# Head transposes six pieces behind their block, and the second attention's multiplication four steps behind its scores

## The chip, the cores and the metric

The kernel runs on one core of a Trainium2 chip. The metric is the device time of one execution in microseconds, given as the median of several runs. In the profile PE is TensorE's matmuls, PEld its weight loads, DVE is VectorE, ACT is ScalarE, POOL is GpSimd, and SP is SyncE, whose queue issues nearly all DMAs.

## What is computed

One encoder block over 256 tokens of width 1024, in float32. The reference, cut to what matters:

```python
h = rmsnorm(x, norm_mix_g)
qkv_a, q_b, k_b, v_b, gate_logits = split(h @ w_in)             # 7424 columns
for gi, (window, dil) in enumerate(((128, 1), (512, 4), (2048, 16))):   # mixer A, 8 heads of 64 each
    qg = partial_rope(rmsnorm(q[gi], qn_a[gi]), pos)
    kg = partial_rope(rmsnorm(k[gi], kn_a[gi]), pos)
    og, lg = dilated_window_attention(qg, kg, v[gi], window, dil)
o_a = sum over groups, weighted by softmax of the denominators
o_b = gqa_blocked_attention(axial_rope(rmsnorm(q_b)), axial_rope(rmsnorm(k_b)), v_b)   # mixer B, 8 on 2 heads
merged = sigmoid(g_a) * (o_a @ w_proj_a) + sigmoid(g_b) * (o_b @ w_proj_b)
x = x + merged @ w_out
x = x + moe_ffn(rmsnorm(x, norm_ffn_g), ...)     # top 4 of 32 experts: 1024 -> 2 x 1024 -> 1024, clamped SwiGLU
```

The experts' weights are 32 x (1024 x 2048 + 1024 x 1024) floats, 402.7 MB; the other matrices are some 42 MB. Each weight is read once.

## The kernel before

**Two parts.** A front part normalises, projects, runs both attentions, merges and routes. Then a loop over 32 experts (line 1266) multiplies the gathered tokens of each expert with its weights as they arrive.

**Steps.** All matmuls with weights in the front part are cut into 76 pieces (lines 840 to 845), one a step. `prep` (line 464) splits a piece's weights into a high and a low part, one ScalarE copy and one VectorE subtraction (`split`, line 375, lines 376 and 377), two steps ahead of use; `run_piece` (line 860) multiplies. The blocks of w_in come in the order v0 kvb k0 q0 k1 q1 k2 q2 v2 v1 qb, four pieces of two 128-rows each (steps 0 to 43; lines 501, 502 and 504 are the matmuls), then 16 gate pieces (44 to 59), 8 projection pieces (60 to 67, lines 489, 490 and 492) and 8 of w_out (68 to 75).

**Tasks.** Everything else is a task with a due step. `later(d, fn)` (line 449) sets one d steps ahead; `run_tasks` (line 453), called ahead of each piece (lines 943 to 956), runs those that are due, in the order of due step and number. So an engine's order is the program's order, written out by steps.

**Key and query heads.** When a key or query block of mixer A is through, `headnorm` (line 511) evicts its two token halves on ScalarE (lines 520 and 521), sums squares on VectorE (522), takes the root on GpSimd (525) and applies the rotary tables there (530 to 535). LAT - 1 steps later VectorE scales each half (line 549), and LAT steps later `qk_epilogue` (line 558) has `transpose_heads` (551) run four 128x128 transposes for each half on TensorE (554) with one ScalarE eviction (555). After the second half the work tile `hn` is dropped (line 568). LAT is 5 (line 509). The heads of mixer B have counts of their own, LATQ and LATK.

**Attentions.** `unit_a` and `unit_b` (lines 657 and 720) each return three tasks: scores with their softmax, transposes of the probabilities (line 640, evicted at 641), and the multiplication with v (`pv`). `schedule_units` (line 769) sets them LAG = (0, 2, 3) steps behind the unit's start. Mixer B's eight units start at steps 53 to 60; its `pv` acts for every second unit, at steps 57, 59, 61 and 63 (line 758). After the fourth and the eighth unit `finish_o` (line 649) evicts the result as a high part on ScalarE (654) and a low part on VectorE (655); the projection of mixer B (pieces 64 to 67) reads it. From step 59 on ScalarE also runs two sigmoids a step for the gates (line 787), and switches its function table between them and the exponentials (line 741).

**Buffers and weights.** Large tiles come from 9 pairs of 1 MB halves (`bigt`, line 135, takes the half that has been free longest; `drop`, line 151, gives back). `pump` (line 299) issues weight loads on SP's queue in order whenever a half is free, at most three chunks ahead until the first attention is done and without a limit after that; a load waits in that queue until the last user of its half is through. The first 20 chunks of the experts are 1 MB each and are fetched in the order FETCH (line 28); they are consumed in the order 0, 1, 2, ... where two neighbours that share a pair give it back together. A later chunk needs a whole pair.

Of the kernel before, what the change touches and what calls it, by code (L numbers as in the profile page):

```python
# [24 lines left out]
N_PAIR, N_ONE = 9, 6  # L25
HALVED, LENT = 2, (1, 2)
BD = 8
FETCH = (1, 12, 4, 16, 6, 5, 2, 3, 10, 7, 11, 13, 0, 14, 15, 8, 17, 9, 18, 19)
RA, RB = 0.7, 1
WU = (6, 10, 2, 0, 0)  # L30
CAP2 = 3
LAG = (0, 2, 3)
W = (2, 1, 2, 4)
SENT = -3.0e38
MARK = 3.0e38
# [44 lines left out]
def hybrid_moe_block(ctx: ExitStack, tc: tile.TileContext, x, norm_mix_g, w_in, b_gate, qn_a, kn_a, qn_b, kn_b,  # L80
# [54 lines left out]
    def bigt(shape, dt=F32, name="b"):  # L135
        n = -(-math.prod(shape[1:]) // SLOT)
        part = [(a, p) for p in halves if p[2] == dt for a, v in zip(p[3], p[1]) if v is None]
        stamp[0] += 1
        age, p = min(part, key=lambda t: t[0], default=(0, None))
        if n == 2 or not part:  # L140
            assert n_pairs[0] < N_PAIR, (name, step, nxt, use, reserve)
            n_pairs[0] += 1
            age, p = 0, [big.tile([128, 2 * SLOT], dt, name=nm(name), tag="big"), [None, None], dt, [0, 0]]
            halves.append(p)
        h = next(i for i in range(2) if p[1][i] is None and p[3][i] == age)
        p[1][h:h + n] = [True] * n
        t = view(p[0][:, h * SLOT:(h + n) * SLOT], shape)
        where[id(t)] = (t, p, h, n)
        return t

    def drop(*tiles):
        for t in tiles:
            _, p, h, n = where.pop(id(t))
            if p is None:
                n_ones[0] -= 1
                continue
            p[1][h:h + n] = [None] * n
            p[3][h:h + n] = [stamp[0]] * n
            if p[1] == [None, None]:
                halves[:] = [q for q in halves if q is not p]  # L160
                n_pairs[0] -= 1
# [10 lines left out]
    def ps(tag, shape=(128, 512), name=None):  # L172
        bufs = {"g": 3, "s": 2, "t": 2, "o": 1}[tag]
        return psum.tile(list(shape), F32, name=nm(tag), tag=tag, bufs=bufs)
# [116 lines left out]
    fetch = list(range(len(chunks)))  # L291
    fetch[n_dense:n_dense + len(FETCH)] = [n_dense + i for i in FETCH]
    nxt = [0]
# [152 lines left out]
    tasks = []  # L446
    step = [0]

    def later(d, fn):
        uid[0] += 1  # L450
        tasks.append((step[0] + d, 10 + uid[0], fn))
# [54 lines left out]

    kqT = {}
    vt = {}
    LAT, LATQ, LATK = 5, 9, 8

    def headnorm(pss, nh, t1_, t2_, rot, dst, post, lat=LAT):

# [35 lines left out]
    def scaled(c, y, r, nh):  # L548
        V.tensor_mul(y, y, r[:, :, None].to_broadcast([128, nh, HD]))

    def transpose_heads(src, dst, nblk):
        pt = ps("t")
        for j in range(nblk):
            PE.transpose(pt[:, j * 128:(j + 1) * 128], src[:, j * 128:(j + 1) * 128], ident)
        S.activation(dst, pt[:, :nblk * 128].rearrange("p (j t) -> p j t", j=nblk), AF.Copy)


    def qk_epilogue(which, g):
        def ep(pss):
            if g not in kqT:  # L560
                kqT[g] = bigt([128, 2, 4, T], name="kqT")
            w = 0 if which == "q" else 1

            def post(c, y, hn):
                later(LAT, lambda: transpose_heads(y.rearrange("p h d -> p (h d)"),
                                                   kqT[g][:, w, :, c * 128:(c + 1) * 128], 4))
                if c == 1:
                    later(LAT, lambda: drop(hn))
            headnorm(pss, 8, lambda c: tabA1[:, w, g, c, :], lambda c: tabA2[:, w, g, c, :], 8,
                     lambda c, y, r: scaled(c, y, r, 8), post)  # L570
        return ep
# [194 lines left out]
                    reserve[0] -= 2  # L766
        return scores, lambda: softmax_t(st), pv

    def schedule_units(units, first, every):
        for n, u in enumerate(units):  # L770
            for j in (0, 2, 1):
                tasks.append((step[0] + first + int(n * every) + LAG[j], (2, 0, 1)[j] + 1000000, u[j]))


    gates = {}
# [107 lines left out]
    units_b = [unit_b(i, c) for c in range(2) for i in range(4)]  # L883
    units_a = [unit_a(hp, c, u) for c in range(2) for hp in range(4) for u in range(2)]
    A0, B0 = max(at["v", 1], at["v", 2]) + 2, at["gate", 0] + 9
# [5 lines left out]
    later(14, rstd_row)  # L891
    later(22, fold_router)
    later(18, expert_bias)
    schedule_units(units_a, A0, RA)
    schedule_units(units_b, B0, RB)
    later(at["proj", 0, 0], hT_done)
    for j in range(8):
        later(at["proj", 0, 0] + j - 1, lambda j=j: gate_sigmoid(j))
# [44 lines left out]
    for i in range(NP + AHEAD - 2):  # L943
# [10 lines left out]
        j = step[0] = i - AHEAD  # L954
# [45 lines left out]
    first = Pair()  # L1000
# [265 lines left out]
    for e in range(n_exp):  # L1266
        p = e // 2
# [34 lines left out]
    with tc.If(most > CAP):  # L1302
        with tc.For_i(0, E, 1) as e:
# [11 lines left out]
            for blk in range(1, T // CAP):  # L1315
# [8 lines left out]
                xT, y = fxy[:, 0, :512].rearrange("p (k s) -> p k s", k=8), fxy[:CAP, 1]  # L1324
# [66 lines left out]
```

## Time and profile before

| | us |
|---|---|
| three runs | 1206.65, 1202.38, 1204.87 |
| median | 1204.87 |
| the profiled execution, its own time | 1208.11 |
| its span | 1206.3 |
| TensorE matmul busy | 1131.8 (94%) |
| VectorE busy | 394.7 (33%) |
| ScalarE busy | 270.6 (22%) |
| GpSimd busy | 104.4 (9%) |
| HBM read 444.01 MB | 369 GB/s over the span |

The span is what the profile covers; the time of the execution is 1.8 us longer. Matmuls overlap, so a busy TensorE is not one at its peak. A row of the timeline gives the start and the length of a group of instructions, its engine and line, the tiles written and read, the shape and count, and in brackets how long the engine stood before it and for what. The clock is the share of TensorE's full speed that was granted.

### The profile page before, as it was taken

The page shows a single profiled execution, that of the slowest core. Times are in us where ns is not written, and L with a number is a line of the kernel's source. Part 1 is how long each engine was busy: PE and PEld are TensorE (multiplying, and loading weights), DVE is VectorE, ACT ScalarE, POOL GpSimd, SP SyncE. Part 2 cuts the span into 40 slices and gives each one's busy share as a digit, 9 for nine tenths or more (in the row PEclk, how much of TensorE's full clock was granted, in tenths as well). Part 3 has the DMA queues.
Part 4 walks back from the last instruction along what each step waited for, and adds up shares of the span by engine and source line. Part 5 has one row for each costly group of instructions (what it writes and reads, how often), then busy time and mean ns, then how long its engine had stood idle before and what let it go on. Part 6 is the DMA issues. An engine that isn't in the chain of part 4 may idle for free.

```text
span 1206.3 us, 14307 instructions
## 1 busy us (share of the span) xinstructions
PE 1131.8 (94%) x5956; PEld 573.5 (48%) x5956; DVE 394.7 (33%) x845; ACT 270.6 (22%) x473; POOL 104.4 (9%) x119
## 2 busy tenths in 40 slices
PE   8999999999999999999989898989898989899996
PEld 6777789897434344343434242324243423233333
DVE  4766576564223222232222131212222222222122
ACT  5644555763111101111011101010101010101011
POOL 4767140010000000000000000000000000000000
PEclk9999999999999999999999999999999999999999
DMA  8724417389999999999999999999999999999995
GB/s 302 267 105 154 160 37 277 143 318 373 399 430 430 430 430 432 429 431 432 430 431 430 431 430 430 431 432 429 431 429 432 431 430 431 430 431 431 430 429 205
DMA packets 59628, 446.03 MB, mean 370 GB/s; under 512 B 5356, under 2 KB 17928, under 8 KB 33928
## 3 DMA queue, kind: packets, MB, share of 16 engines
q1 hardware_dynamic: 59224, 444.41, 88.8%
q8 instruction: 49, 0.80, 0.2%
q10 hardware_dynamic: 336, 0.66, 0.2%
q14 instruction: 19, 0.16, 0.0%
HBM read 444.01 MB, written 1.05 MB: 369 GB/s over the span
## 4 chain that ended last, share of the span: by engine, by line
DMA 49%; PE 38%; POOL 6%; issue 3%; ACT 3%; DVE 2%; ACTq 0%; POOLq 0%; SPq 0%; DVEq 0%
DMA w<-in_w_down_dram 26%; DMA w<-in_w_gate_up_dram 23%; PE g L1137 14%; PE o L1177 6%; PE s L1195 2%; PE g L489 2%; PE g L490 2%; PE g L492 2%; POOL hrs L525 1%; PE s L1110 1%; PE t L1157 1%; POOL w L530 1%; PE g L502 1%; PE g L501 1%; POOL hz L533 1%
## 5 line engine op out<-in xcount | busy, mean ns | idle before, releaser
L1137 PE MATMUL g<-w,pair 128*64 128x512 f32 x2008 | 450.5, 596 | 26.9 <-DMA w<-in_w_gate_up_dram 26.0
L1137 PEld LDWEIGHTS g<-w,pair 128*64 128x64 f32 x2008 | 137.9, 137 | 310.6 <-issue 264.9
L1177 PE MATMUL o<-w,act 128*64 128x512 f32 x992 | 222.1, 596 | 27.7 <-DMA w<-in_w_down_dram 27.6
L1160 DVE TENSOR_TENSOR gu<-t,biasT 128x256 f32<-128x256 f32 x128 | 45.4, 417 | 428.1 <-PE t L1157 428.1
L1177 PEld LDWEIGHTS o<-w,act 128*64 128x64 f32 x992 | 70.0, 137 | 167.0 <-issue 117.4
L1147 ACT ACTIVATE gu<-g 128x512 f32<-128x512 f32 x64 | 38.2, 597 | 408.9 <-PE g L1137 399.7
L1185 ACT ACTIVATE pair<-o 64x512 f32<-64x512 f32 x62 | 36.6, 591 | 283.3 <-PE o L1177 282.8
L1112 DVE TENSOR_TENSOR pair<-s,gT 128x512 f32<-128x512 f32 x30 | 20.8, 692 | 184.8 <-PE s L1110 184.8
L377 DVE TENSOR_TENSOR whl<-w,whl 128x1024 fp32r<-128x1024 f32 (+1 forms) x60 | 73.7, 1254 | 18.3 <-ACT whl L376 17.9
L501 PE MATMUL g<-whl,hTh 128*128 128x512 f32 (+1 forms) x176 | 70.0, 400 | 0.7 <-ACT whl L376 0.5
L502 PE MATMUL g<-whl,hTh 128*128 128x512 f32 (+1 forms) x176 | 68.4, 391 | 0.0
L1110 PEld LDWEIGHTS s<-selr,xa 128*128 128x128 f32 x480 | 57.7, 196 | 12.2 <-issue 12.2
L1110 PE MATMUL s<-selr,xa 128*128 128x128 f32 x480 | 60.5, 285 | 0.0
L376 ACT ACTIVATE whl<-w 128x1024 fp32r<-128x1024 f32 (+1 forms) x60 | 59.7, 1039 | 2.6 <-PE g L504 1.7
L1195 PE MATMUL s<-pair,gT 128*128 128x512 f32 x120 | 56.9, 606 | 0.0
L1196 DVE TENSOR_TENSOR acc<-s,acc 128x512 f32<-128x512 f32 x56 | 38.7, 692 | 29.9 <-PE s L1195 29.9
L504 PE MATMUL g<-whl,hTh 128*128 128x512 f32 (+1 forms) x176 | 45.9, 383 | 0.0
L1157 PEld LDWEIGHTS t<-cf,gu 128*128 128x128 f32 x256 | 33.3, 210 | 26.0 <-issue 26.0
L1157 PE MATMUL t<-cf,gu 128*128 128x128 f32 x256 | 39.4, 297 | 0.0
L501 PEld LDWEIGHTS g<-whl,hTh 128*128 128x128 f32 x176 | 33.9, 193 | 8.7 <-ACT whl L376 1.3
L502 PEld LDWEIGHTS g<-whl,hTh 128*128 128x128 f32 x176 | 34.0, 193 | 6.1
L504 PEld LDWEIGHTS g<-whl,hTh 128*128 128x128 f32 x176 | 32.9, 192 | 6.7
(280 smaller groups left out, 981.6 us busy)
## 6 DMA issues: line engine op xcount, KB each, us to landing
w<-in_w_gate_up_dram SPq DMA_DIRECT2D x120, 2048.0 KB, 38.8
w<-in_w_down_dram SPq DMA_DIRECT2D x60, 2048.0 KB, 38.7
w<-in_w_in_dram SPq DMA_DIRECT2D x22, 1024.0 KB, 8.3
w<-in_w_gate_up_dram SPq DMA_DIRECT2D x11, 1024.0 KB, 9.4
w<-in_w_down_dram SPq DMA_DIRECT2D x6, 1024.0 KB, 9.6
w<-in_w_in_dram SPq DMA_DIRECT2D x6, 512.0 KB, 8.3
P<-in_w_in_dram SPq DMA_DIRECT2D x3, 1024.0 KB, 6.3
P<-in_w_gate_up_dram SPq DMA_DIRECT2D x3, 1024.0 KB, 7.7
```

The source lines that it names most:

```text
L376: S.activation(dst_h, src, AF.Copy)
L377: V.tensor_sub(dst_l, src, f(dst_h))
L501: PE.matmul(pss[c][:, :n], lh[:, k, cols], h[:, q, :], start=(k == 0), stop=False)
L502: PE.matmul(pss[c][:, :n], ll[:, k, cols], h[:, q, :], start=False, stop=False)
L504: PE.matmul(pss[c][:, :n], lh[:, k, cols], l[:, q, :], start=False, stop=(k == nk - 1))
L1110: PE.matmul(pg[:, j * 128:(j + 1) * 128], xa[:, c, run_cols(k, GU)], q.selr[:, c].rearrange("p a s -> p (a s)"), start=(c == 0), stop=(c = ...
L1137: PE.matmul(g1[j][u * 64:(u + 1) * 64, :], a, w[:, k - k0, u * FF + j * 512:u * FF + (j + 1) * 512], start=(k == 0), stop=(k == 7))
L1157: PE.transpose(pt[:, j * 128:(j + 1) * 128], gu[:, run_cols(k, DN)], ident)
L1160: V.tensor_add(t[:, 4 * b:4 * b + 4, :], p4[:, :, u, :], bias[:, u * 8 + 4 * b:u * 8 + 4 * b + 4, :].to_broadcast([128, 4, CAP]))
L1177: PE.matmul(po[u * 64:(u + 1) * 64, :], act[:, k, :], w[:, k - k2, u * 512:(u + 1) * 512], start=(k == 0), stop=(k == 7))
L1195: PE.matmul(pc, q.gT[:, c * 128:(c + 1) * 128], q.ysb[:, sl], start=True, stop=True)
L1196: V.tensor_add(acc[0][:, c, sl], pc, base[:, c, sl])
```

## The change

The transposes of mixer A's key and query heads, their evictions and the freeing of `hn` come six steps behind the block (a new constant LATT); the scaling in front of them keeps its step. The multiplications of mixer B come four steps behind the unit's start (58, 60, 62 and 64); mixer A's stay at three. Eight of the 20 entries of FETCH stand in another order.

```diff
-FETCH = (1, 12, 4, 16, 6, 5, 2, 3, 10, 7, 11, 13, 0, 14, 15, 8, 17, 9, 18, 19)
+FETCH = (1, 2, 4, 16, 6, 3, 5, 12, 10, 7, 11, 13, 0, 14, 15, 8, 17, 9, 18, 19)
-LAG = (0, 2, 3)
+LAG = ((0, 2, 3), (0, 2, 4))
...
-    LAT, LATQ, LATK = 5, 9, 8
+    LAT, LATT, LATQ, LATK = 5, 6, 9, 8
...
             def post(c, y, hn):
-                later(LAT, lambda: transpose_heads(y.rearrange("p h d -> p (h d)"),
+                later(LATT, lambda: transpose_heads(y.rearrange("p h d -> p (h d)"),
                                                    kqT[g][:, w, :, c * 128:(c + 1) * 128], 4))
                 if c == 1:
-                    later(LAT, lambda: drop(hn))
+                    later(LATT, lambda: drop(hn))
...
-    def schedule_units(units, first, every):
+    def schedule_units(units, first, every, lag):
         for n, u in enumerate(units):
             for j in (0, 2, 1):
-                tasks.append((step[0] + first + int(n * every) + LAG[j], (2, 0, 1)[j] + 1000000, u[j]))
+                tasks.append((step[0] + first + int(n * every) + lag[j], (2, 0, 1)[j] + 1000000, u[j]))
...
-    schedule_units(units_a, A0, RA)
-    schedule_units(units_b, B0, RB)
+    schedule_units(units_a, A0, RA, LAG[0])
+    schedule_units(units_b, B0, RB, LAG[1])
```

## Rows read from the trace of the kernel before

**Rows 1.** Busy us by engine in two stretches, granted clock, DMA share, GB/s.

```profile
295.00:300.00 5.00, 5.00 (x26) 1.72 (x24) 0.00 (x0) 0.00 (x0) 0.00 (x0) 1.00 0.66 213
540.00:1190.00 650.00, 595.46 (x2796) 230.06 (x2794) 144.07 (x331) 72.16 (x124) 0.00 (x0) 1.00 1.01 429
```

**Rows 2.** SP queue's own waits, 0 to 330 us: sum, times, longest.

```profile
SPq L314 <- PE g L1137: 24.1, 6, 7.8
```

**Rows 3.** Timeline of TensorE, head transposes (L554) and ends of weight pieces (L504).

```profile
54.69 0.63 PE L554 MATMUL t<-cf,w 128*128 128x128 f32 x4 [1.14 <-DVE w L549]
...
82.72 0.63 PE L554 MATMUL t<-cf,tabs 128*128 128x128 f32 x4 [0.85 <-DVE tabs L549]
84.43 0.63 PE L554 MATMUL t<-cf,tabs 128*128 128x128 f32 x4 [1.08 <-DVE tabs L549]
...
95.80 1.03 PE L554 MATMUL t<-cf,w 128*128 128x128 f32 x8
...
101.22 1.07 PE L504 MATMUL g<-whl,hTh 128*128 128x512 f32 x4
103.94 1.07 PE L504 MATMUL g<-whl,hTh 128*128 128x512 f32 x4
...
108.35 0.63 PE L554 MATMUL t<-cf,w 128*128 128x128 f32 x4 [0.63 <-PE g L504]
110.12 0.63 PE L554 MATMUL t<-cf,w 128*128 128x128 f32 x4 [1.14 <-DVE w L549]
```

**Rows 4.** Busy us by engine around three waits; the third number from the end is the clock.

```profile
52.00:55.00 3.00, 1.86 (x12) 1.29 (x11) 1.98 (x3) 2.38 (x5) 1.74 (x4) 1.00 0.00 1
107.00:115.00 8.00, 6.24 (x25) 4.67 (x24) 6.77 (x8) 6.23 (x9) 5.72 (x5) 0.79 0.74 249
234.00:242.00 8.00, 6.20 (x44) 5.46 (x43) 4.76 (x9) 7.91 (x14) 0.00 (x0) 0.79 0.00 0
```

**Rows 5.** Timeline of GpSimd, head normalisation of blocks k0, k2 and q2.

```profile
47.42 1.29 POOL L530 TENSOR_TENSOR w<-w,tabs 128x512 f32<-128x512 f32 x1
...
50.00 2.28 POOL L530 TENSOR_TENSOR w<-w,tabs 128x512 f32<-128x512 f32 x1
...
98.97 3.97 POOL L525 TENSOR_TENSOR hrs<-hss,mhalf 128x16 f32<-128x16 f32 x1 [3.65 <-DVE hss L524]
...
111.45 3.85 POOL L525 TENSOR_TENSOR hrs<-hss,mhalf 128x16 f32<-128x16 f32 x1 [2.20 <-DVE hss L524]
```

**Rows 6.** Timeline of VectorE, the two scalings of block k2.

```profile
106.49 1.76 DVE L549 TENSOR_TENSOR w<-w,hrs 128x512 f32<-128x512 f32 x1 [1.04 <-POOL w L535]
109.28 0.69 DVE L549 TENSOR_TENSOR w<-w,hrs 128x512 f32<-128x512 f32 x1 [1.03 <-POOL w L535]
```

**Rows 7.** Timeline of TensorE, multiplication of units 4 and 5 (L758), projection halves (L492).

```profile
234.80 0.43 PE L758 MATMUL o<-P,vb 128*64 128x128 f32 x2
237.03 1.88 PE L758 MATMUL o<-P,vb 128*64 128x128 f32 x14 [1.80 <-ACT P L641]
...
248.06 0.64 PE L492 MATMUL g<-oT,whl 128*128 128x256 f32 x4
249.50 0.64 PE L492 MATMUL g<-oT,whl 128*128 128x256 f32 x4
```

**Rows 8.** DMA issues by tile: count, KB each, median us to landing.

```profile
w<-in_w_in_dram SPq DMA_DIRECT2D x22, 1024.0 KB, 8.3
```

**Rows 9.** Timeline of VectorE: low part of the first result, last unit's scaling.

```profile
229.65 0.69 DVE L655 TENSOR_TENSOR oT<-o,oT 128x512 fp32r<-128x512 f32 x1 [1.85 <-ACT oT L654]
...
239.54 0.62 DVE L745 TENSOR_SCALAR tabs<-tabs,mzb 128x256 f32<-128x256 f32 x2
```

**Rows 10.** Timeline of ScalarE: first result's eviction, table loads for units 6 and 7.

```profile
229.03 0.59 ACT L654 ACTIVATE oT<-o 128x512 fp32r<-128x512 f32 x1
231.02 1.28 ACT L741 ACT_TABLE_LOAD   x1 [1.40 <-DVE mzb L739]
...
237.00 1.28 ACT L741 ACT_TABLE_LOAD   x1
```

## The prediction, on record before the result

> **What bounds the kernel now.** I read the stretches first. From 540 to 1190 us the DMA engines are full (share 1.01, 429 GB/s) while TensorE stands 54 of 650 us [rows 1]: the experts' 402.7 MB set that part, and a change in front of it pays only if it brings forward the moment from which the weights run without a break. That moment hangs on TensorE: the last break is at 295 to 300 us (213 GB/s, so 2.5 us of weights lost) [rows 1], and the DMA queue's own waits show why: it stood six times, 24.1 us in all, until the first experts' matmuls gave buffers back [rows 2]. So the front part, up to the first expert matmul, counts nearly one to one as long as TensorE paces it. There I read TensorE's timeline for what it stands for, and find two places that the diff touches.
>
> The first is the query/key heads. A weight piece of 512 columns takes 2.72 us (101.22 to 103.94) [rows 3]. The head transposes of the three key blocks wait for VectorE's scaling: 1.14 us at 54.69, 0.85 and 1.08 at 82.72 and 84.43, 0.63 and 1.14 at 108.35 and 110.12 [rows 3]; the eight at 95.80, of a query block, ran in one go behind key block k2's last matmul. After the third wait the clock fell: 0.79 over 107 to 115, a loss of (1 - 0.79) x 8 = 1.68 us, from the 2.4 to the 1.2 GHz level and back; after the first it did not (1.00 over 52 to 55) [rows 4]. What they wait for is GpSimd: block k2 starts there at 98.97 and ends when VectorE's last scaling can start, at 109.28 [rows 5, 6].
>
> The second is the second attention. Its third probability multiplication starts at 234.80, stands 1.80 us for ScalarE's eviction of transposed probabilities, and goes on at 237.03 [rows 7]; over 234 to 242 the clock is 0.79, again 1.68 us [rows 4].
>
> **Part 1, LATT 5 to 6.** Twelve groups of transposes (two token halves of six blocks), their ScalarE evictions and the freeing of hn move one piece later; their count does not change. The scaling stays where it is (lat is unchanged), so VectorE's and GpSimd's order stays. Removed: the waits, 1.14 + 0.85 + 1.08 + 0.63 + 1.14 = 4.84 us; per key block another 0.23 because two groups of four (0.63 each) become one of eight (1.03), so 0.69; and the clock's 1.68. That is 7.2 us.
>
> What is late next: k2's heads are ready some 14.2 us after its block's last matmul: 3.2 from 95.80 until GpSimd starts at 98.97, 10.3 on GpSimd until 109.28, 0.69 of scaling [rows 3, 5, 6]. Five pieces and one block's transposes give 5 x 2.72 + 0.8 = 14.4: covered, by 0.2. A query block's reductions stand behind the key block's last scaling in VectorE's order, so its GpSimd work starts 2.2 us after the key block's (the wait at 111.45) [rows 5]: ready 14.2 + 2.2 + 10.3 = 26.7 after the key block's end, against nine pieces and two blocks' transposes, 26.1. I leave 0.6 us of waiting in sum. Bounds: nothing left (-7.2), or only the one piece won (-2.7, a rival below). Taken: **-6.6 us**, since GpSimd's dates come forward with the matmuls that feed it.
>
> ScalarE: the evictions now stand one weight split later; nobody waits on them but the scores of step 38, a whole piece (2.72) after q2's transposes. SP: hn's slot comes free one piece later, and two w_in chunks are loaded into such slots (those for steps 30 and 42); they land 8.3 us after issue [rows 8], and six or more steps (over 16 us) lie between. Following bigt, drop and pump by hand, every w_in chunk gets the slot that it had. Cost: nothing; if that cover were gone, up to one piece.
>
> **Part 2, LAG of the second attention 3 to 4.** The four multiplications move from steps 57, 59, 61, 63 to 58, 60, 62, 64. Removed: the wait of 1.80 and the clock's 1.68 at step 61, 3.48 us. Step 61 goes straight from 234.8 into its piece, two halves of 1.44 (248.06 to 249.50) [rows 7], and is through at 237.7.
>
> Added, first: step 62 opens with the transposes of the last unit's probabilities, and these are scaled only at 239.54 + 0.62 = 240.16 [rows 9]. Does this date come forward? ScalarE is the pace there: one round from one exponential's table load to the next takes 237.00 - 231.02 = 5.98 us [rows 10]. The move takes the eviction of 0.59 at 229.03 and the 1.40 that the exponentials stood (they waited for a reduction queued on VectorE behind L655) out of step 59 [rows 9, 10], and puts both into step 60, in front of the last unit's exponentials: unit 6 gets 2 us earlier, unit 7 stays. So TensorE, which came to these transposes behind that date before, now stands **2.5 us** (237.7 to 240.16), with the third multiplication and the piece of step 62 queued behind. Bounds 0.5 (both ScalarE savings reach unit 7) to 2.7.
>
> Second: the last multiplication stands at step 64, right in front of the first projection that reads its result. From the eviction's start to the end of the low part on VectorE is 229.03 to 229.65 + 0.69, 1.31 us [rows 9, 10], with the hand-overs **1.4 us**, which before lay beside step 63's piece. Bounds 1.3 to 2.5 (a weight split of one us ahead on ScalarE).
>
> The clock: two waits. The only long ones of the trace, 1.77 in two parts and 1.80, cost 1.68; those of 1.14 and of 0.85 with 1.08 cost nothing [rows 3, 4]. I let it fall after the 2.5 (1.68) and not after the 1.4. Bounds 0 and 3.36. Part 2: 2.5 + 1.4 + 1.68 - 3.48 = **+2.1 us**.
>
> **Part 3, FETCH and the slots.** P slots come free one step later, so the prefetched expert chunks choose other slots. By hand: chunk 1 as before; chunk 2 takes the slot of the first projection chunk, 4 and 16 the slots that they had, then 6, 3, 5, 12, 10, and the pairs end as (2,3), (4,5), (6,7), (10,11), (12,13), each with both halves consumed together. Before step 64 is over, eight one-MB chunks are issued either way; the last four depend on step 64's multiplication instead of 63's and come within some 0.5 us of their old place, with over 10 us of transfers queued in front of them. Zero; if the cover fails, 1 MB at 429 GB/s, 2.4 us, which the break at 295 us could hold [rows 1].
>
> **Sum.** -6.6 + 2.1 = -4.5 us in the profiled execution (span 1206.3, own time 1208.11: 1203.6). The median of the runs, 1204.87, is 3.2 below that execution; I put the same sum on it: **1200.4**.
>
> **Rivals.** (a) *GpSimd keeps the pace*: only latency is bought, its blocks keep their dates, and by step 38 TensorE is ahead by the one piece put before the last transposes: -2.7 + 2.1, 1204.3. For it: GpSimd works 2 x 10.3 us in a pair of blocks, and waits of 2.2 and 3.65 us are its only gaps [rows 5]. Against: the 3.65 is a wait for the matmuls. (b) *The second attention costs nothing*: no clock fall, 2.5 + 1.4 - 3.48 = +0.4, so -6.2, 1198.7. For: waits of 1.14 left the clock alone. Against: 2.5 is the longest of all. (c) *The gain stops at the weights*: if the chunks' dates do not follow, only the 2.5 us break closes: 1202.4. Against: the queue's waits are for matmuls [rows 2]. (d) *Slower: GpSimd stretches*. Its 512-wide multiply took 1.29 at 47.42 and 2.28 at 50.00 [rows 5], and VectorE's scaling 1.76 at 106.49 beside a busy GpSimd, 0.69 at 109.28 beside an idle one [rows 6]: they hinder each other. If splits now fall beside both multiplies of a block, that is 2.0 us a block, 8.0 over k1, q1, k2, q2, all of it waited for: -6.6 + 8.0 + 2.1 = +3.5, 1208.4. It decides from 1.1 us a block (4.5 / 4). Against: VectorE's order is unchanged, and k2 took its 10.3 us with splits beside it. The Trainium skill, GPSIMD Engine Reference, section 1 (Specifications), speaks for (d): GpSimd's SBUF interfaces are shared with VectorE and contend with VectorE instructions that have two SBUF inputs; by that rule, these rows agree.
>
> **Numbers.** Forecast 0.47 (1198.9 to 1202.0), (b) 0.20, (a) 0.17, (c) 0.08, (d) 0.08. Range 1197.4 to 1204.4: it leaves out (d), a part of (a), and the far side of (b). About 0.3%, 3.6 us, is what a measurement of this kernel tells from no change, so 1201.25 is the line: of the forecast 0.7 lies beyond it, of (b) nearly all, of (a) and (c) little: faster 0.54; slower 0.08 from (d); same 0.38.
>
> **What would show it.** Right: no VectorE waits over 0.5 us at L554, granted clock 1.00 through 107 to 115, the scores of step 38 some 6 to 7 us earlier; a wait of about 2.5 us at the last unit's transposes instead of 1.8 at a multiplication, 1.4 us at step 64, the first expert matmul some 4.5 us earlier. Wrong: GpSimd's blocks at their old dates (a), clock 1.00 past step 62 (b), a longer break of the DMA around 295 (c), GpSimd blocks over 11.4 us (d).

## The result and the profile after

| | median | runs | ratio to before, 95% |
|---|---|---|---|
| before | 1204.72 us (1202.38 to 1206.65) | 6 | |
| after | 1196.32 us (1195.35 to 1199.64) | 6 | 0.9934 [0.9923, 0.9946] |
| before, later | 1202.22 us (1201.39 to 1205.66) | 11 | |
| after, later | 1196.44 us (1196.18 to 1198.26) | 6 | 0.9946 [0.9932, 0.9960] |

The change is worth 8.0 us (1 - 0.9934 of 1204.7), with 6.5 to 9.3 in the interval, and 6.5 us in the later comparison, with 4.8 to 8.2 in the interval; the two medians of after agree within 0.2 us, so what differs is before's. The forecast was 4.5 us. The median lies 1.1 us under the low end of the range; the sign was right.

The two first profiles may not be subtracted. Their spans differ by 12.0 us (1206.3 and 1194.3), of which 3.5 lie behind the first expert matmul, where both kernels stream the same weights, and the profile of before is of an execution in which TensorE's clock fell more often than in others, as the experiments show below. First what the profile after shows at the places of the prediction.

TensorE at the head transposes, timeline of after:

```profile
54.84 1.03 PE L554 MATMUL t<-cf,w 128*128 128x128 f32 x8
70.81 1.03 PE L554 MATMUL t<-cf,w 128*128 128x128 f32 x8
82.91 1.03 PE L554 MATMUL t<-cf,tabs 128*128 128x128 f32 x8
95.01 1.03 PE L554 MATMUL t<-cf,w 128*128 128x128 f32 x8
107.16 1.03 PE L554 MATMUL t<-cf,w 128*128 128x128 f32 x8
...
118.93 1.03 PE L554 MATMUL t<-cf,w 128*128 128x128 f32 x8
```

Against [rows 3]: the eight transposes of each of the six blocks run in one go, and no wait stands behind them in brackets. All five waits are gone.

Busy time by engine of after, the stretches of [rows 4] and then those around the break of the weights, [rows 1] (after the window and its length: PE, PEld, DVE, ACT, POOL, then the granted clock, DMA share, GB/s):

```profile
107.00:115.00 8.00, 8.00 (x41) 6.72 (x40) 5.38 (x7) 4.06 (x6) 7.32 (x6) 1.00 0.54 165
234.00:242.00 8.00, 6.89 (x63) 6.32 (x62) 5.47 (x6) 7.97 (x15) 0.00 (x0) 1.00 0.68 213
285.00:290.00 5.00, 5.00 (x27) 1.74 (x27) 1.33 (x6) 0.56 (x1) 0.00 (x0) 1.00 0.53 152
290.00:295.00 5.00, 5.00 (x26) 1.59 (x24) 1.59 (x12) 0.64 (x2) 0.00 (x0) 1.00 0.97 390
295.00:300.00 5.00, 5.00 (x26) 1.72 (x24) 0.82 (x4) 1.08 (x2) 0.00 (x0) 1.00 1.00 411
300.00:305.00 5.00, 5.00 (x28) 2.19 (x26) 1.38 (x5) 0.12 (x1) 0.00 (x0) 1.00 1.00 423
305.00:310.00 5.00, 5.00 (x26) 1.63 (x24) 2.99 (x9) 1.91 (x2) 0.00 (x0) 1.00 0.94 374
```

The clock is 1.00 in both stretches where it was 0.79. The break of the weights has come forward with the first expert matmul and is still there (152 GB/s at 285 to 290), so TensorE still paces the moment from which the weights run.

GpSimd, timeline of after, the starts of q1, k2 and q2's norms:

```profile
83.43 3.85 POOL L525 TENSOR_TENSOR hrs<-hss,mhalf 128x16 f32<-128x16 f32 x1 [2.20 <-DVE hss L524]
...
95.51 3.85 POOL L525 TENSOR_TENSOR hrs<-hss,mhalf 128x16 f32<-128x16 f32 x1 [2.20 <-DVE hss L524]
...
107.60 3.85 POOL L525 TENSOR_TENSOR hrs<-hss,mhalf 128x16 f32<-128x16 f32 x1 [2.20 <-DVE hss L524]
```

k2 starts at 95.51, in [rows 5] at 98.97, 3.5 us earlier, of which 1.1 were there at the first block already (k0 starts at 42.41, in before at 43.47). So GpSimd's dates came forward, and its wait of 3.65 us in front of k2 shrank to 2.20.

The second attention, TensorE's timeline of after: the last unit's transposes, the third multiplication, the last one, and the two waits at step 64:

```profile
231.38 0.63 PE L640 MATMUL t<-cf,w 128*128 128x128 f32 x4
231.93 1.09 PE L758 MATMUL o<-P,vb 128*64 128x128 f32 x16
...
238.91 1.09 PE L758 MATMUL o<-w,vb 128*64 128x128 f32 x16
...
240.70 0.39 PE L489 MATMUL g<-oT,whl 128*128 128x256 f32 x1 [0.70 <-ACT oT L654]
...
241.49 0.39 PE L490 MATMUL g<-oT,whl 128*128 128x256 f32 x1 [0.41 <-DVE oT L655]
```

Step 64 waits 1.11 us by the brackets, near the 1.4 of the forecast. The 2.5 us in front of the transposes at 231.38 are missing: the piece's last group of four started at 230.68, and such a group is followed after 0.48 (227.37 to 227.85 at the transposes before), so TensorE stood some 0.2 us.

ScalarE's timeline of after shows why, with the reduction of VectorE beside it:

```profile
221.81 1.28 ACT L741 ACT_TABLE_LOAD   x1
...
227.68 0.59 ACT L654 ACTIVATE oT<-o 128x512 fp32r<-128x512 f32 x1
228.28 1.28 ACT L741 ACT_TABLE_LOAD   x1
229.62 0.48 ACT L741 ACTIVATE w<-s,mzb 128x256 f32<-128x256 f32 x1
```

```profile
228.90 0.68 DVE L739 TENSOR_REDUCE mzb<-s 128x2 f32<-128x512 f32 x1
...
230.88 0.62 DVE L745 TENSOR_SCALAR w<-w,mzb 128x256 f32<-128x256 f32 x2
```

The eviction of 0.59 did move in front of the last unit's exponentials, as forecast: one round is now 228.28 - 221.81 = 6.47 us, 0.49 longer than the 5.98 of [rows 10]. The 1.40 us did not lengthen it. In [rows 10] the table load itself waited for the reduction (231.02, [1.40 <-DVE mzb L739]) and the exponential came 1.28 behind that. Here the load starts at 228.28, 0.6 before the reduction starts, and when the reduction ends at 229.58 the table is there: the exponential starts at 229.62.

The two programs say what differs. ScalarE's instructions for unit 6 and what each waits for, before and then after (DVE is VectorE, Activation is ScalarE itself, and the number is the semaphore's; x2 is for the two halves of the unit):

```
L741 ACT_TABLE_LOAD [waits DVE_49]
L741 ACTIVATE tabs_90,mzb_2210<-s_2204,mzb_2210 128x256 [waits Activation_49] x2
```

```
L741 ACT_TABLE_LOAD
L741 ACTIVATE w_1911,mzb_2200<-s_2194,mzb_2200 128x256 [waits DVE_49]
L741 ACTIVATE w_1911,mzb_2200<-s_2194,mzb_2200 128x256
```

Before, unit 6's P lay in a half of the pair of `tabs` that had held the first chunk of the projection's weights, and the last instructions to read that chunk on ScalarE were its splits (line 376). So the exponential had two things to wait for, VectorE's reduction and ScalarE's own split, and the wait for the reduction stood in front of the table load. Unit 7's P lay in the same pair behind it; its exponential waited for the reduction alone, and its load ran free (237.00 in [rows 10], without a bracket). After, expert chunk 2 takes that half, as the forecast found by hand in its part 3. Units 6 and 7 got another pair, the exponential has one thing to wait for, and the load waits for nothing. That the slot decides this is read from the programs; the experiments move the load itself, not the slot.

### The profile page after: what moved, and what is told of

It reads as the page before. It is cut to its first block, busy times and chain, and to the rows that moved or that the text cites. A ratio compares the mean times of both kernels' runs of the same rounds, so it can differ in the third digit from the quotient of the medians.

```text
span 1194.3 us, 14307 instructions
## 1 busy us (share of the span) xinstructions
PE 1130.4 (95%) x5956; PEld 571.4 (48%) x5956; DVE 394.6 (33%) x845; ACT 270.4 (23%) x473; POOL 106.1 (9%) x119
## 4 chain that ended last, share of the span: by engine, by line
DMA 47%; PE 42%; POOL 5%; issue 2%; DVE 2%; ACT 2%; ACTq 0%; SPq 0%; POOLq 0%; DVEq 0%
DMA w<-in_w_gate_up_dram 23%; DMA w<-in_w_down_dram 22%; PE g L1137 16%; PE o L1177 7%; PE s L1195 2%; PE g L489 2%; PE s L1110 2%; PE g L490 2%; PE g L492 2%; POOL hrs L525 1%; PE t L1157 1%; POOL w L530 1%; PE g L504 1%; PE g L501 1%; PE g L502 1%
## 5 line engine op out<-in xcount | busy, mean ns | idle before, releaser
L1137 PE MATMUL g<-w,pair 128*64 128x512 f32 x1992 | 447.0, 597 | 26.5 <-DMA w<-in_w_gate_up_dram 25.5
L1137 PEld LDWEIGHTS g<-w,pair 128*64 128x64 f32 x1992 | 137.1, 137 | 307.7 <-issue 263.3
L504 PE MATMUL g<-whl,hTh 128*128 128x512 f32 (+1 forms) x176 | 46.3, 386 | 0.0
L504 PEld LDWEIGHTS g<-whl,hTh 128*128 128x128 f32 x176 | 32.8, 191 | 6.7
```

The lines of the kernel that those rows point to most:

```text
L504: PE.matmul(pss[c][:, :n], lh[:, k, cols], l[:, q, :], start=False, stop=(k == nk - 1))
L1137: PE.matmul(g1[j][u * 64:(u + 1) * 64, :], a, w[:, k - k0, u * FF + j * 512:u * FF + (j + 1) * 512], start=(k == 0), stop=(k == 7))
```

## Two more profiles of before

The forecast took 3.36 us of clock from one execution. So before was profiled again, unchanged, twice.

> The kernel before, profiled once more, for its clock. If the clock always falls behind the waits at the key heads (107 to 115 us) and at the multiplication of line 758 (234 to 242 us), as the forecast took it, the granted clock is again 0.79 in both stretches, and the span within 1 us of 1206.3. If those falls belong to some executions only, one or both stretches show 0.9 or more, and the span is shorter by the 1.7 us of each that is missing.

> The kernel before, profiled a third time. The waits are the same as in the two profiles so far (at the key heads 1.1, 0.9, 1.1, 0.6 and 1.1 us; 1.8 at line 758). If the clock's falls are a matter of the execution and not of the waits alone, the stretches 107 to 115 and 234 to 242 us show 0.79 in one and 1.00 in another execution again: of the four executions with the heads five pieces behind, two fell in the first stretch; of the four with the wait of 1.8 us, one fell in the second. If they always fall, 0.79 in both and a span within 1 us of 1206.3.

The stretches 60 to 67, 107 to 115 and 234 to 242 us of the second execution of before (span 1201.9), and then of the third (span 1202.5):

```profile
60.00:67.00 7.00, 7.00 (x31) 5.67 (x30) 3.42 (x5) 0.00 (x0) 5.72 (x8) 0.76 0.00 0
...
107.00:115.00 8.00, 6.27 (x32) 4.88 (x31) 6.75 (x9) 7.20 (x10) 5.72 (x6) 1.00 0.71 248
...
234.00:242.00 8.00, 6.82 (x62) 6.65 (x63) 3.51 (x7) 7.94 (x15) 0.00 (x0) 1.00 0.12 24
```

```profile
60.00:67.00 7.00, 7.00 (x39) 5.97 (x38) 3.42 (x5) 0.00 (x0) 5.61 (x8) 1.00 0.00 0
...
107.00:115.00 8.00, 7.01 (x26) 5.75 (x27) 6.49 (x8) 5.53 (x8) 5.79 (x4) 0.79 0.49 168
234.00:242.00 8.00, 7.17 (x53) 6.84 (x54) 3.50 (x8) 7.94 (x14) 0.00 (x0) 0.79 0.17 43
```

One kernel, the same waits (1.14, 0.84, 1.08, 0.60 and 1.13 us at the key heads and 1.79 at line 758 in the second), and each of the three falls is there in one execution and not in another. So a fall does not belong to its wait for good, and one execution cannot price it. All executions together, from the start times of four instructions: a is from the start of GpSimd's first block (L525 of k0) to the first scores of step 38 (L674), b from the first scores of the second attention (L732) to the first expert matmul (L1137), c from there to the end of the span.

| kernel | a | clock falls in a, near | b | fall in b | c |
|---|---|---|---|---|---|
| before, first | 86.08 | 60 and 107 | 92.17 | yes | 912.6 |
| before, second | 84.70 | 60 | 91.40 | no | 910.8 |
| before, third | 84.46 | 107 | 92.13 | yes | 911.0 |
| second attention alone (e2) | 84.71 | 60 | 90.59 | no | 910.3 |
| before with early table (e5) | 84.50 | 107 | 90.28 | no | 912.4 |
| heads alone (e1) | 78.60 | none | 91.43 | no | 911.1 |
| after, first | 80.22 | 60 | 90.62 | no | 909.1 |
| after, second (e9) | 80.20 | 60 | 90.59 | no | 909.7 |
| after, old order of weights (e3) | 80.17 | 60 | 90.60 | no | 912.9 |
| after, table load held back (e4) | 78.60 | none | 92.13 | no | 910.2 |
| after, 20 matmuls more (e7) | 78.60 | none | 92.68 | no | 910.2 |
| after, last one at step 63 (e6) | 80.23 | 60 | 89.71 | no | 910.3 |
| the same (e10) | 80.23 | 60 | 89.67 | no | 913.1 |

Where the clock falls alike, a and b repeat within 0.06 us; c does not, it moves by up to 2.8 us between executions of one kernel (e6 and e10). In a and b the table reads the change to a tenth of a microsecond where the runs' times cannot.

The DMA records say where c moves. From the first expert matmul until 440 of the 446 MB had moved it took 882.4 to 882.8 us in twelve of the thirteen executions, before and after alike, and 886.2 in e3. The rest, from there to the end, is 26.5 to 30.5 us. So a microsecond that the first expert matmul comes earlier is kept through the whole stream, and the 3.5 us of c between the two first profiles lie in the last 30 us. That last part was 26.5 to 27.8 us in seven of the eight executions with the later multiplication (30.5 in e10) and 28.2 to 30.1 in the five without it; whether the change has a hand in it no run here tests.

## The experiments

**e1, the heads alone** (LATT 6; second attention and FETCH as before).

```diff
-    LAT, LATQ, LATK = 5, 9, 8
+    LAT, LATT, LATQ, LATK = 5, 6, 9, 8
...
-                later(LAT, lambda: transpose_heads(y.rearrange("p h d -> p (h d)"),
+                later(LATT, lambda: transpose_heads(y.rearrange("p h d -> p (h d)"),
...
-                    later(LAT, lambda: drop(hn))
+                    later(LATT, lambda: drop(hn))
```

> The kernel before with the head transposes alone moved one piece later (LATT 6); the second attention and FETCH are as before. Theory (the heads carry most of the gain: their waits of 4.8 us and the clock's fall at 110 us are gone, and the second attention gives the rest): 5.5 to 7 us faster than before, 1197.7 to 1199.2; no VectorE wait at L554, clock 1.00 from 107 to 115, and at the second attention the old wait of 1.8 us at L758 with the clock's fall behind it. Rival (the prediction's step that the second attention costs 2.1 us in the changed kernel): then the heads alone give more than the whole change, 10 us, 1194 to 1195.

1198.31 us, ratio 0.9948 [0.9935, 0.9961]: 6.3 us (4.7 to 7.8), so the rival's 10 us are out. No head transpose waits. Against the second execution of before, which fell at 60 like the first profile of after, a is 84.70 - 80.22 = 4.5 us shorter, and that is the waits: from the first head transposes to the scores (49.0 to 127.7 us) TensorE was idle 4.81 us in that execution of before, and 0.06 us in the same work of e1. The fall near 107 costs 86.08 - 84.70 = 1.4 us; it came in three of five executions with the heads five pieces behind and in none of eight with six, so on average 0.8 goes with it, a share from few executions. The heads are worth **5.3 us**.

TensorE's timeline of e1 has the old wait of the second attention; behind it the clock is 1.00, and a second wait that the first profile of before does not have comes with it:

```profile
229.35 1.09 PE L758 MATMUL o<-P,vb 128*64 128x128 f32 x14 [1.80 <-ACT P L641]
...
237.56 1.09 PE L758 MATMUL o<-tabs,vb 128*64 128x128 f32 x14 [0.39 <-ACT tabs L641]
```

When the clock does fall, TensorE arrives later at the second place and does not stand there: a fall in b costs 92.17 - 91.40 = 0.77 us, not 1.68. The stand is longer than its bracket of 0.38 or 0.39. In the second execution of before, the last multiplication and the half piece behind it take 2.90 us from start to start (242.57 to 245.47), without a wait 2.08 (245.98 to 248.06 in the first): 0.8 us, and that much of the 1.68 is hidden.

**e2, the second attention alone** (LATT 5; multiplications four steps behind, new FETCH).

```diff
-FETCH = (1, 12, 4, 16, 6, 5, 2, 3, 10, 7, 11, 13, 0, 14, 15, 8, 17, 9, 18, 19)
+FETCH = (1, 2, 4, 16, 6, 3, 5, 12, 10, 7, 11, 13, 0, 14, 15, 8, 17, 9, 18, 19)
-LAG = (0, 2, 3)
+LAG = ((0, 2, 3), (0, 2, 4))
```

> The changed kernel with the head transposes put back to five pieces (LATT 5): the second attention's lag of four steps and the new FETCH alone. Theory: 1 to 3 us faster than before, 1201.7 to 1203.7: the 1.8 us wait at L758 and the clock's fall (1.68) are gone, and about 1.1 us at step 64 plus some tenths at the last transposes come instead. Rival (the prediction's sum): 2.1 us slower than before, 1206.8, with 2.5 us of waiting at the last unit's transposes and a clock fall behind it.

1202.31 us, ratio 0.9984 [0.9969, 0.9998]: 1.9 us faster, where the forecast of this part alone was 2.1 us slower. b is 0.8 us shorter than in the second execution of before, without a fall in either. ScalarE's table load for the last unit, and TensorE at the transposes:

```profile
233.32 1.28 ACT L741 ACT_TABLE_LOAD   x1
234.66 0.47 ACT L741 ACTIVATE w<-s,mzb 128x256 f32<-128x256 f32 x1
```

```profile
236.42 0.63 PE L640 MATMUL t<-cf,w 128*128 128x128 f32 x4
```

No wait stands at the transposes; the two at step 64 are those of after (0.70 and 0.41). The load starts ahead of the reduction (233.95 to 234.63) without the heads' part too, so it comes from the later multiplication and the slots that it frees later.

**e4, the table load held back.** After, with a copy of two numbers on ScalarE in front of the last unit's exponentials. The copy waits for the reduction, so the load behind it does too; the column that it writes is written again before it is read.

```diff
+            if c == 1 and i == 3:
+                S.activation(mz[:, 1, :], mz[:, 0, :], AF.Copy)
             for u in range(2):
```

> The changed kernel with one two-element ScalarE copy of the reduction's result in front of the last unit's exponentials, so that their table load of 1.28 us starts only behind the reduction, as unit 6's did in the kernel before. Nothing is left out. Theory (what the prediction missed is that the table load runs while the reduction is still out, so the last unit's probabilities come 1.7 us earlier than forecast): the wait at the last unit's transposes grows from 0.2 to about 1.7 us; 1.5 us slower than the changed kernel, 1197.8, and about 3.2 slower, 1199.5, if the clock falls behind it. Rival (TensorE simply arrives later than forecast, the table load does not matter): within 0.5 us of the changed kernel.

ScalarE and then TensorE of e4:

```profile
228.74 0.20 ACT L741 ACTIVATE mzb<-mzb 128x2 f32<-128x2 f32 x1 [1.35 <-DVE mzb L739]
228.97 1.28 ACT L743 ACT_TABLE_LOAD   x1
```

```profile
232.01 0.63 PE L640 MATMUL t<-cf,w 128*128 128x128 f32 x4 [1.57 <-DVE w L747]
```

With the load behind the reduction a wait is there, at the transposes that the forecast named: 1.57 us by its bracket, and 229.81 to 232.01 from start to start, 1.7 more than the 0.48 without a wait. b is 92.13, 1.5 us longer than in after and 0.7 longer than in before without a fall. So the later multiplication alone, with its table load held, would have lost 0.7 us. The forecast's terms without any clock are 2.5 + 1.4 - 1.80 = 2.1. The clock did not fall behind this wait. The time, 1197.89 us and ratio 0.9943 [0.9930, 0.9956], is 1.1 us over the first ratio of after, and the intervals overlap: the profile decides here, not the time.

**e5, the same load taken out of its wait in the kernel before.**

```diff
+            if c == 1 and i == 2:
+                S.activation(mz[:, 1, 0:1], mhalf[:, 0:1], AF.Exp)
             for u in range(2):
```

> The kernel before, with one exponential of a single column on ScalarE ahead of unit 6's exponentials in the second attention; the column of mz that it writes is not read. The exponentials' table is then loaded while VectorE still works at the reduction, instead of 1.28 us behind it. Theory (what the change gained in the second attention is that unit 7's table load no longer stands behind the reduction): the same load taken out of its wait in the kernel before brings unit 6's exponentials and ScalarE's eviction of its transposed probabilities some 1.3 us forward, so the wait of 1.80 us at the multiplication of line 758 falls to about 0.5, and the time by 1.2 us; by up to 2.9 if the clock falls behind that wait. Rival (the gain is that of the later multiplication, and the load only went along): the wait stays within 0.3 us of 1.80 and the time is that of the kernel before within 0.5 us.

ScalarE and then TensorE of e5:

```profile
227.40 1.28 ACT L741 ACT_TABLE_LOAD   x1
228.69 0.20 ACT L741 ACTIVATE mzb<-mhalf 128x1 f32<-128x1 f32 x1
228.93 0.47 ACT L743 ACTIVATE tabs<-s,mzb 128x256 f32<-128x256 f32 x1
```

```profile
233.65 1.09 PE L760 MATMUL o<-P,vb 128*64 128x128 f32 x14 [0.66 <-ACT P L641]
```

The wait at the multiplication falls from 1.79 to 0.66 and b from 91.40 to 90.28, by 1.1 us, as the theory says; the rival's unchanged 1.80 is refuted. 1202.98 us, ratio 0.9987 [0.9974, 1.0000]: 1.6 us, with nothing at the end of the interval. This one line gets from the kernel before, in b, 0.3 us more than the later multiplication does (90.28 against 90.6).

**e3, the old order of the weights in the kernel after.**

```diff
-FETCH = (1, 2, 4, 16, 6, 3, 5, 12, 10, 7, 11, 13, 0, 14, 15, 8, 17, 9, 18, 19)
+FETCH = (1, 12, 4, 16, 6, 5, 2, 3, 10, 7, 11, 13, 0, 14, 15, 8, 17, 9, 18, 19)
```

> The changed kernel with the old order of the first 20 expert chunks. With the slots of the changed kernel, two pairs then hold chunks of different experts (5 with 12, 3 with 13), so that 4 MB come free some 14 us later than they could. Theory (FETCH only repairs the pairs): slower than the changed kernel by 3 to 9 us (4 MB are 9.8 us at 429 GB/s, less what TensorE's own pace hides), seen as a longer DMA break behind the first expert matmul. Rival (the order is worth nothing, the DMA catches up): within 1 us of the changed kernel, 1195.3 to 1197.3. Second rival (the new order brings part of the gain by itself): also slower, but with the break of the DMA unchanged and the first expert matmul later.

The break of the weights in e3, stretch by stretch, to be read against the same stretches of after:

```profile
290.00:295.00 5.00, 5.00 (x26) 1.60 (x24) 1.11 (x9) 0.64 (x2) 0.00 (x0) 1.00 0.83 356
295.00:300.00 5.00, 5.00 (x26) 1.72 (x24) 1.30 (x7) 0.60 (x1) 0.00 (x0) 1.00 0.83 288
300.00:305.00 5.00, 5.00 (x28) 2.10 (x24) 0.83 (x3) 0.60 (x1) 0.00 (x0) 1.00 1.00 403
305.00:310.00 5.00, 5.00 (x26) 1.72 (x24) 3.25 (x10) 1.91 (x2) 0.00 (x0) 1.00 0.61 200
```

a and b are those of after. In these 20 us 6.2 MB moved (5 us of 356, 288, 403 and 200 GB/s), in after 8.0: 1.75 MB, of which 0.24 (0.55 us) goes back to the first expert matmul's being 0.55 us later in this execution. The other 1.5 MB are 3.5 us at 429 GB/s, and from the first expert matmul to 440 MB it takes 886.2 us against 882.5 and 882.6 in the two executions of after. (c as a whole, 912.9 against 909.1 and 909.7, would not show it: e10 has 913.1 with the new order.) By time it is 1199.71 us, ratio 0.9958 [0.9945, 0.9971]: 2.9 us over the first ratio of after and 1.4 over the second. So the new order earns nothing against before, whose 440 MB come at the same 882.5 to 882.7 us, but without it the changed kernel's stream is some 3.5 us late.

**e7, a delay in front of the weights.** After, with 20 matmuls more.

```diff
-W = (2, 1, 2, 4)
+W = (2, 1, 22, 4)
```

> The kernel after, with 20 matmuls of 256 columns more, whose results are not read, in front of the second half of the first experts' gather: 20 at the 0.11 us that the two in that place take one after the other, 2.2 us of TensorE more ahead of the first expert matmul, which comes that much later. Theory (the first expert matmul paces the weights, one to one): 2.2 us slower than the kernel after (2.0 to 2.5), and the break of the weights' stream longer by as much. Rival (c) of the prediction (what is gained in front of the weights closes only a part of their break, so a loss opens only a part): 1.1 us or less.

TensorE's timeline of e7, then the break:

```profile
282.23 2.57 PE L1067 MATMUL t<-cb 128*128 128x256 bf16 x22
...
286.61 1.94 PE L1137 MATMUL g<-P,pair 128*64 128x512 f32 x8
```

```profile
285.00:290.00 5.00, 5.00 (x31) 2.69 (x31) 2.25 (x8) 0.00 (x0) 0.00 (x0) 1.00 0.28 55
290.00:295.00 5.00, 5.00 (x26) 1.60 (x24) 0.66 (x6) 0.32 (x1) 0.00 (x0) 1.00 0.84 344
```

The matmuls cost 2.1 us (b 92.68 against 90.62). From the start to 30 us behind the first expert matmul 73.0 MB had moved, in after 73.1: no byte came early for the delay, and 440 MB were through 882.8 us behind that matmul, in after 882.5. So the delay goes through to the stream, one to one within 0.3 us. The time, 1198.25 us, ratio 0.9947 [0.9929, 0.9964], lies 1.6 us above the first ratio of after and level with the second; it cannot tell 2.1 from 1.1 by itself.

**e6 and e10, the last multiplication back at step 63**, in the kernel after.

```diff
-                tasks.append((step[0] + first + int(n * every) + lag[j], (2, 0, 1)[j] + 1000000, u[j]))
+                tasks.append((step[0] + first + int(n * every) + lag[j] - (lag[j] == 4 and n == 7),
+                              (2, 0, 1)[j] + 1000000, u[j]))
```

> The kernel after, with the last of the second attention's four multiplications back at step 63 (three steps behind the scores), the three before it still four behind. The order of the weights' loads is that of the kernel after. Theory: the multiplication was behind the last unit's transposes by a whole piece (2.7 us) already at step 63, so it waits for nothing there, and the output's eviction and low part then lie beside step 63's piece: the wait of 0.7 and 0.4 us at step 64 goes, and the time is 1.1 us under that of the kernel after (bounds 0.5 and 1.3). Rival: ScalarE is late with the last transposed probabilities, so the multiplication at step 63 waits 0.5 us or more and the time is that of the kernel after within 0.4 us.

> The kernel after with the last of the second attention's multiplications back at step 63, beside the kernel after on the same chip. From the first scores of the second attention to the first expert matmul the profile showed 89.7 us for it and 90.6 for the kernel after; by the theory that the weights run one to one with that moment, it is 0.9 us faster (0.5 to 1.3), which 5 rounds can just not tell from nothing. Rival (0.9 us there is lost again in the weights' stream): the same time within 0.3 us, and fewer bytes moved in the 30 us behind the first expert matmul.

> The kernel after, timed once more on the chip of the next run, as its comparison, and profiled once more for the clock. Theory (with the key heads six pieces behind, TensorE no longer stands there, so its clock does not fall there): granted clock 1.00 over 107 to 115 us, as in the six executions with this setting so far; over 60 to 67 us, which the change does not touch, 0.76 or 1.00. Rival (the fall at 107 to 115 comes by chance in some executions of either kernel): under 0.9 there.

TensorE's timeline of e6 has the last multiplication at 236.94, without a wait, and none at L489 or L490 behind it:

```profile
236.94 1.64 PE L758 MATMUL o<-w,vb 128*64 128x128 f32 x16
```

b is 89.71 and 89.67, 0.9 us under the kernel after in both executions: the two waits at step 64 are gone. By time e6 has 1196.32 us, ratio 0.9930 [0.9910, 0.9949], and e10 1196.20 us, 0.9941 [0.9927, 0.9954], beside 0.9946 [0.9932, 0.9960] for the kernel after on the same chip (e9). Both ratios lie a little under those of the kernel after (0.9934 and 0.9946), but neither tells 0.9 us from nothing, since c alone moves by up to 2.8. In e9 the clock is 1.00 over 107 to 115 and 0.76 over 60 to 67, the theory's side.

## Why the prediction was wrong

The heads, part 1, were forecast at -6.6 us and are worth -5.3. The second attention, part 2, was forecast at +2.1 and is worth -1.2. So the miss is in part 2, 3.3 us, and 1.3 of it were covered by part 1.

The steps of the forecast, with what the table and the timelines give, in us:

| step | forecast | found |
|---|---|---|
| waits at the key heads | -4.84 | -4.8 |
| two groups of four become one of eight | -0.69 | 0 (within 0.3) |
| waits left over | +0.6 | 0 |
| clock near 107 | -1.68 | -0.8 |
| wait of 1.80 at step 61 | -1.80 | -1.8 |
| clock behind it | -1.68 | -0.4 |
| wait of 0.38 at the last multiplication | not seen | -0.4 |
| **wait at the last unit's transposes** | **+2.5** | **+0.2** |
| **clock behind that** | **+1.68** | **0** |
| step 64 | +1.4 | +1.1 |
| left over, so that a gives -4.5 and b -0.8 before clock | | +0.4 |
| FETCH and slots | 0 | 0 |
| sum | -4.5 | -6.5 |

The found ones are taken with each fall's share of the executions: 1.4 us in three of five, 0.77 in two of the four with the wait of 1.8 us. Their sum, 6.5 us, lies within both intervals of the kernel after; it is at the edge of the first. Whether the rest of the first 8.0 us is anything but spread stays open; the last 30 us of the span are where it could lie.

The waits are the brackets', and a bracket can count less than TensorE loses: it starts at the modelled end of the matmuls in front of it. From start to start, against places without a wait, b has no remainder: -2.2 for the wait at step 61 (232.96 to 237.25 in the second execution of before, against 2.1 without a wait), -0.8 at the last multiplication, +0.2 at the transposes, +1.4 at step 64 (238.91 to 242.43 in after, against 2.1), and +0.6 where transposes are now followed by another group instead of a piece. By this count the forecast's 1.4 for step 64 was right.

**The step that failed** is the one on ScalarE: the eviction of 0.59 and the 1.40 that the exponentials stood were both put "into step 60, in front of the last unit's exponentials: unit 6 gets 2 us earlier, unit 7 stays". Only the eviction lengthened the round. The wait for the reduction came along (228.28 to 229.58, 1.30 us), but not in front of the table load: the load of 1.28 filled it. In before the load had stood behind the reduction, by the programs because of the slot in which unit 6's P lay. The forecast had the two ends ("0.5 (both ScalarE savings reach unit 7) to 2.7") and took the wrong one; the 0.2 found lies even under the lower. I had followed by hand which slots the weights' chunks get, and not what the slots of P mean for ScalarE's waits. e4 puts the hold back, and with it 1.5 of the 2.3 us that are missing. Of the other 0.8, 0.4 are that TensorE reaches these transposes later than forecast: at 238.1 and not 237.7, put on before's axis by the first scores of this attention (201.57 and 194.60). The rest is not placed.

**The second step** is the clock. A fall of 1.68 us behind the longest wait was added because the one profile had falls behind its two longest waits. It had a third, which the forecast did not see, over 60 to 67 us, behind the window of 52 to 55 that it read. After has that fall as well, with TensorE busy all through the 16 us in front of it (46 to 62). The first profiles of before and then of after:

```profile
60.00:67.00 7.00, 7.00 (x32) 5.65 (x31) 3.69 (x6) 0.00 (x0) 6.14 (x9) 0.76 0.00 0
```

```profile
60.00:67.00 7.00, 7.00 (x27) 5.66 (x27) 4.39 (x5) 0.00 (x0) 4.94 (x8) 0.76 0.04 14
```

Thirteen executions show that this is no rule: waits of 1.8 us with a fall (before, first and third) and without (before, second; e1), and 1.57 without (e4). The heads' clock term was over-counted by the same reasoning, in the other direction, so the errors nearly cancelled: the three clock terms add up to -1.7 in the forecast and to -1.2 as found. That is luck.

**What held.** The heads' mechanism: no wait at L554, clock 1.00 over 107 to 115, and of the 4.8 us of waits a got 4.5 shorter. (The 0.63 among them is put down to TensorE itself in [rows 3], not to VectorE; VectorE's scaling of that half ended at 106.49 + 1.76 = 108.25 [rows 6], 0.1 before the transposes, and with the later transposes the wait is gone like the others.) The scores of step 38 came 6.9 us earlier between the two first profiles (129.55 to 122.63), inside the 6 to 7 forecast, though 1.1 of that was there before k0's block and 1.4 was the fall near 107. Step 64's wait. The weights follow the first expert matmul, though the stretch at 295 to 300 us was not their last dip: at 315 to 320 before still ran at 329 GB/s. FETCH costs nothing against before; but its bound, 2.4 us, was too small for what the old order would have cost (3.5), and the text did not say that the order is what makes the term zero. The grouping term was double counting: the idle time in brackets ends where the second group starts, and the groups' own 0.63 us hold a modelled end that overlaps the next matmul.

**The rivals.** (a) GpSimd did not keep its dates: k2 started 3.5 us earlier, 2.4 counted from k0's start. (b) The second attention costs nothing, -6.2 in all, was the nearest, and right that no fall follows; but it kept the 2.5 us of waiting that did not come, and its +0.4 was in truth -1.2. (c) The gain did not stop at the weights: e7's delay goes through, and 440 MB come the same 882.5 to 882.7 us behind the first expert matmul in before and in after. (d) GpSimd did not stretch: its pair of blocks takes 107.60 - 83.43 = 24.2 us, 12.1 for a half with 2.20 us of waiting in it, against 111.45 - 98.97 = 12.5 for a half in [rows 5], with 2.20 as well.

## What to carry to other kernels

A wait that the profile puts on a table load, or on any instruction that needs no data, says that the load could go first. Ask why the wait does not stand on the instruction behind it, and free the load, with one small instruction of the same table ahead (e5), or with another slot, which here was read from the programs and not tried by itself. When work moves by a step, follow the slots that its tiles get on every engine that writes them, not only the transfers into them. And price a fall of the clock from several executions, as a share, or leave it in the range: one profile shows that it can happen, not that it does.

## What the runs showed of the hardware

ScalarE's table load of 1.28 us runs beside VectorE's reduction when nothing is put in front of it, and the exponential follows 0.04 us after the reduction's end (229.58 to 229.62). Where nothing else is waited for, the instruction behind a load starts 1.29 to 1.30 us after the load's start (227.40 to 228.69 in e5; 221.81 to 223.11 for unit 6 in after). The Trainium skill, ScalarE: Activation LUTs, section What ACT_TABLE_LOAD costs, gives about 1283 ns for the load, with which the 1.28 agrees, and a drain of some 1380 ns on top for each switch. These rows have no room for the second: in after the eviction ends at 228.27, the load starts at 228.28, and the table is there when the reduction ends at 229.58. The granted clock after a stall is not a function of the stall: in one kernel, over 60 to 67 us, behind the same work, it was 0.76 in two executions and 1.00 in the third, and with the heads at five pieces each of the five executions fell near 60 or near 107, one at both. None of the eight executions without the waits at the heads fell near 107.
